# Column sums of a 256 MB array: eight running rows with one VectorE add a load and a small GpSimd add, in place of four running rows with two VectorE adds a load

## The chip, the cores and the metric

The kernel runs on one core of a Trainium2 chip. The metric is the device time in microseconds of one execution. The engines that matter here are VectorE (DVE in the profile), GpSimd (POOL), TensorE (PE) and ScalarE (ACT); SyncE (SP) computes nothing and issues the transfers from HBM to SBUF.

## The reference

```python
batch, seq, dim = 32, 1024, 2048
grad_output = np.random.randn(batch, seq, dim).astype(np.float32)

def reference(grad_output):
    return np.sum(grad_output, axis=(0, 1)).astype(np.float32)
```

The input is 32768 rows of 2048 float32 numbers, 268.4 MB. The result is one row of 2048 column sums. Every byte is read once, and there is one addition for each number read.

## The kernel before

**Tiling.** SBUF has 128 partitions. A *row group* is 128 input rows, one on each partition, 2048 columns wide (1.05 MB); the input has 256 row groups. Three ring slots (`ring`, `SLOTS`) of 128 x 16384 columns hold eight row groups each (`M`). All loads go through the one queue of SP, in the order in which the program issues them (`load`, line 57). A load into a slot waits until the instructions that use the slot's old content are done; the framework places these semaphore waits, and the order of the instructions on each engine is the order of the program (`tc.manual_schedule()`).

**The chain (lines 90 to 99).** There are 29 loads of eight row groups (8.39 MB each), into slots 0, 1, 2, 0 and so on. The running sum is four row groups wide and lives in the first half of the newest slot. For each load VectorE does two adds of 8192 columns by `plus` (line 62): the running sum of the slot before into the first half of the new slot (line 98), and the second half of the new slot into its first half (line 99). The first of the two frees the slot before, into which load i+2 then goes.

**The tail (lines 102 to 135).** After the chain 24 row groups are left: a load of eight into slot s8, one of seven into s7, two of three into parts of the slot `run`, which also holds the running sum, three of one row group without its last 256 columns (line 113, columns up to `C` = 1792), and three of those last 256 columns (line 117). VectorE folds what it has in place by halves (`fold`): the running four rows to one, s8 to one, s7 to two, and one add of two rows of `run`. TensorE then sums over the partitions: `sums` (line 79) is a *row pass*, four matmuls that multiply one row group by a column of ones and add to the PSUM tile `acc`. There are eleven such passes, in a fixed order that ends with the late row groups, and then twelve small matmuls for the last 256 columns into `accr` (line 135).

**The end.** ScalarE copies `acc` to SBUF (line 147), ScalarE and GpSimd copy a part of it each (line 150), VectorE adds `accr` (line 154), and three small transfers store the result.

Of the kernel before, what the change touches and what calls it, by code (L numbers as in the profile page):

```python
# [1 line left out]

# [4 lines left out]

P = 128
M = 8
SLOTS = 3  # L10
CHAIN = 29
B = 256
LATE = 3


@with_exitstack
def kernel(
    ctx: ExitStack,
    tc: tile.TileContext,
    grad_output: bass.AP,  # L20
    out: bass.AP,
):

    nc = tc.nc
    f32 = mybir.dt.float32
    D = out.shape[-1]
    flat = grad_output.rearrange("b s d -> (b s) d")
    Q = D // 4
    H = B // 2
    C = D - B
    add = mybir.AluOpType.add

    sb = ctx.enter_context(tc.tile_pool(name="sb", bufs=1))
    ps = ctx.enter_context(tc.tile_pool(name="ps", bufs=1, space=bass.MemoryType.PSUM))
    ring = [sb.tile([P, M * D], f32, name=f"ring{s}") for s in range(SLOTS)]
    ones = sb.tile([P, 1], f32, name="ones")
    res = sb.tile([P, Q], f32, name="res")
    joint = sb.tile([P, C - 2 * Q], f32, name="joint")
    acc = ps.tile([P, 512], f32, name="acc")
    accr = ps.tile([P, 512], f32, name="accr")
    q, v, t, a, p = nc.sync, nc.vector, nc.tensor, nc.scalar, nc.gpsimd

    row = 0

    def load(s, at, m):

        nonlocal row
        src = flat[row * P : (row + m) * P].rearrange("(p m) d -> p (m d)", p=P)
        q.dma_start(out=ring[s][:, at * D : (at + m) * D], in_=src)
        row += m

    def plus(s, to, n, s2, of):  # L60
        part = ring[s][:, to * D : (to + n) * D]
        v.tensor_tensor(out=part, in0=part, in1=ring[s2][:, of * D : (of + n) * D], op=add)  # L62

    def fold(s, m, left):
        while m > left:
            n = m // 2
            plus(s, 0, n, s, m - n)
            m -= n

    def shares(x):  # L70


        ends = x[:, 2 * Q :].rearrange("p (b g c) -> p g b c", g=2, c=H)
        return [x[:, :Q], x[:, Q : 2 * Q], ends[:, 0], ends[:, 1]]

    def sums(s, at, w=D):
        for g, x in enumerate(shares(ring[s][:, at * D : at * D + w])):
            o = acc[32 * g : 32 * g + 1, : Q if g < 2 else (w - 2 * Q) // 2]
            t.matmul(  # L79
                o if g < 2 else o.rearrange("p (b c) -> p b c", c=H),  # L80
                lhsT=ones[:],
                rhs=x,
                start=False,
                stop=False,
                tile_position=(0, 32 * g),
                skip_group_check=True,
            )

    with tc.manual_schedule():
        for i in range(CHAIN):  # L90
            s = i % SLOTS
            load(s, 0, M)
            if i == 0:
                v.memset(ones[:], 1.0)  # L94
                v.memset(acc[:], 0.0)  # L95
                v.memset(accr[:], 0.0)  # L96
            else:
                plus(s, 0, 4, (i - 1) % SLOTS, 0)
            plus(s, 0, 4, s, 4)


        run, s8, s7 = (s, *((s + k) % SLOTS for k in (1, 2)))
        load(s8, 0, 8)
        fold(run, 4, 1)
        load(s7, 0, 7)
        fold(s8, 8, 1)
        load(run, 4, 3)
        fold(s7, 7, 2)
        plus(run, 4, 1, run, 5)
        load(run, 1, 3)  # L110
        tail = flat[row * P :]
        for k in range(3):
            q.dma_start(
                out=ring[s8][:, (1 + k) * D : (1 + k) * D + C], in_=tail[k * P : (k + 1) * P, :C]
            )
        for k in range(LATE):
            q.dma_start(
                out=ring[s8][:, 4 * D + k * B : 4 * D + (k + 1) * B],
                in_=tail[k * P : (k + 1) * P, C:],
            )  # L120
        sums(run, 6)
        sums(run, 0)
        sums(s8, 0)
        sums(s7, 0)
        sums(s7, 1)
        for at in (1, 2, 3):
            sums(run, at)
        sums(s8, 1, C)
        sums(s8, 2, C)
        sums(run, 4)  # L130
        sums(s8, 3, C)
        for k in range(LATE):
            for g in (2, 3):
                x = 4 * D + k * B + (g - 2) * H
                t.matmul(  # L135
                    accr[32 * g : 32 * g + 1, :H],
                    lhsT=ones[:],
                    rhs=ring[s8][:, x : x + H],
                    start=False,
                    stop=False,  # L140
                    tile_position=(0, 32 * g),
                    skip_group_check=True,
                )

        a.copy(out=res[0:97, :], in_=acc[0:97, :])  # L147
        left = joint[64:65, :].rearrange("p (b g c) -> p g b c", g=2, c=H)
        for g, copy in enumerate((a.copy, p.tensor_copy)):
            copy(  # L150
                out=left[:, g],
                in_=res[64 + 32 * g : 65 + 32 * g, : Q - H].rearrange("p (b c) -> p b c", c=H),
            )
        v.tensor_tensor(  # L154
            out=res[64:97, Q - H :], in0=res[64:97, Q - H :], in1=accr[64:97, :H], op=add
        )
        q.dma_start(out=out[: 2 * Q].rearrange("(g c) -> g c", g=2), in_=res[0:33:32, :])
        a.dma_start(out=out[None, 2 * Q : C], in_=joint[64:65, :])
        q.dma_start(
            out=out[C:].rearrange("(g c) -> g c", g=2), in_=res[64:97:32, Q - H :]  # L160
        )
# [1 line left out]
_INS = ['grad_output']  # L163
_OUTS = [((2048,), 'float32')]


# [23 lines left out]
```

## Time and profile before

| what | value |
|---|---|
| median of 3 runs | 631.58 us (629.75 to 631.66) |
| profiled execution | 630.45 us, of which the span in the trace is 628.7 us |
| VectorE busy | 531.9 us |
| TensorE matmul busy | 13.5 us |
| GpSimd busy | 0.7 us |
| input queue (q1) | 268.44 MB, 99.0% of 16 DMA engines' span |
| VectorE, 128x8192 add | 58 times, 8.69 us each |
| GpSimd, copy of 1x384 | 0.502 us |
| granted TensorE clock | 0.999 |

The span runs from the first to the last instruction of the trace; 1.75 us of the device time lie around it. In a group's line, the numbers behind the bar are the busy time in us, the mean of one instruction in ns, and the time that the engine was idle just before these instructions, with what ended it. A line of the timeline gives the start and the length in us, the engine, the line in the kernel, the operation, and the idle time before it with its releaser. A timeline line with "x4" is several instructions in one, and its length goes from the first to the last of them.

### The profile page before, as it was taken

To read this page: it belongs to the slowest core of one execution; us is meant where nothing else is said; L and a number is where in the kernel's file an instruction comes from. 1 tells how busy PE (TensorE), PEld (TensorE's weight loads), DVE (VectorE), ACT (ScalarE), POOL (GpSimd) and SP (SyncE) were. 2 spreads that over 40 slices of the span, in tenths; PEclk is the share of its full clock that TensorE was granted. 3 is DMA by queue.
4 is the path that set the end of the run, shared out by engine and by line. 5 is a ranking of instruction groups with operands and counts; after the bars stand their busy time and mean duration, and the time that the engine had idled before them with its cause. 6 is when DMAs were issued, how large, how long until landed. Compare 5 with 4: busy or idle time off the path is not lost.

```text
span 628.7 us, 443 instructions
## 1 busy us (share of the span) xinstructions
PE 13.5 (2%) x108; PEld 3.1 (0%) x108; DVE 531.9 (85%) x69; ACT 2.4 (0%) x3; POOL 0.7 (0%) x5
## 2 busy tenths in 40 slices
PE   0000000000000000000000000000000000000026
PEld 0000000000000000000000000000000000000001
DVE  0538988889888899888898888988889988889993
ACT  0000000000000000000000000000000000000000
POOL 0000000000000000000000000000000000000000
PEclk9999999999999999999999999999999999999999
DMA  9999999999999999999999999999999999999996
GB/s 400 404 463 400 467 400 467 400 467 400 467 400 467 400 467 400 467 400 467 400 467 400 467 400 467 401 463 404 463 404 463 404 463 404 459 409 459 413 411 254
DMA packets 5629, 268.48 MB, mean 427 GB/s; under 512 B 629, under 2 KB 1015, under 8 KB 1402
## 3 DMA queue, kind: packets, MB, share of 16 engines
q1 hardware_dynamic: 5624, 268.44, 99.0%
q8 instruction: 1, 0.02, 0.0%
q14 instruction: 2, 0.02, 0.0%
q10 hardware_dynamic: 2, 0.00, 0.0%
HBM read 268.44 MB, written 0.01 MB: 427 GB/s over the span
## 4 chain that ended last, share of the span: by engine, by line
issue 99%; POOLq 0%
POOLq L185 0%; POOLq L174 0%
## 5 line engine op out<-in xcount | busy, mean ns | idle before, releaser
L62 DVE TENSOR_TENSOR ring<-ring 128x8192 f32<-128x8192 f32 (+3 forms) x37 | 287.2, 7769 | 21.8 <-DMA ring<-in_grad_output_dram 20.7
L62 DVE TENSOR_TENSOR ring<-ring,ring 128x8192 f32<-128x8192 f32 x28 | 243.4, 8693 | 64.2 <-DMA ring<-in_grad_output_dram 64.2
L79 PE MATMUL acc<-ring,ones 128*1 128x512 f32 (+1 forms) x96 | 13.1, 688 | 611.3 <-DMA ring<-in_grad_output_dram 609.5
L154 DVE TENSOR_TENSOR res<-res,accr 33x128 f32<-33x128 f32 x1 | 0.3, 293 | 6.4 <-ACT res L147 6.4
L79 PEld LDWEIGHTS acc<-ring,ones 128*1 128x1 f32 x96 | 2.6, 90 | 620.8 <-issue 615.6
L147 ACT COPY res<-acc 97x512 f32<-97x512 f32 x1 | 0.6, 587 | 621.6 <-PE acc L79 621.6
L147 ACT ACT_TABLE_LOAD x1 | 1.3, 1283 | 1.5 <-DVE acc L95 1.5
L150 POOL COPY joint<-res 1x384 f32<-1x384 f32 x1 | 0.5, 502 | 624.6 <-ACT res L147 624.6
L135 PE MATMUL accr<-ring,ones 128*1 128x128 f32 x12 | 0.8, 272 | 0.0
L94 DVE MEMSET ones<- 128x1 f32 x1 | 0.1, 59 | 0.8 <-PEq L174 0.8
L95 DVE MEMSET acc<- 128x512 f32 x1 | 0.5, 485 | 0.1
L135 PEld LDWEIGHTS accr<-ring,ones 128*1 128x1 f32 x12 | 0.5, 84 | 0.5 <-DMA ring<-in_grad_output_dram 0.2
L96 DVE MEMSET accr<- 128x512 f32 x1 | 0.5, 485 | 0.1
L150 ACT COPY joint<-res 1x384 f32<-1x384 f32 x1 | 0.5, 507 | 0.0
L174 POOL MEMSET const-bfloat16-1.0<- 128x1 bf16 x1 | 0.1, 102 | 0.0
L174 POOL MEMSET const-uint8-127<- 128x1 uint8 x1 | 0.1, 100 | 0.0
L174 POOL MEMSET const-float32-0.0<- 128x1 f32 x1 | 0.1, 99 | 0.2 <-issue 0.2
L174 POOL MEMSET const-float32-1.0<- 128x1 f32 x1 | 0.1, 99 | 0.0
## 6 DMA issues: line engine op xcount, KB each, us to landing
ring<-in_grad_output_dram SPq DMA_DIRECT2D x1, 7168.0 KB, 27.5
ring<-in_grad_output_dram SPq DMA_DIRECT2D x2, 3072.0 KB
ring<-in_grad_output_dram SPq DMA_DIRECT2D x3, 896.0 KB, 16.1
ring<-in_grad_output_dram SPq DMA_DIRECT2D x30, 29.9
ring<-in_grad_output_dram SPq DMA_DIRECT2D x3, 128.0 KB, 16.6
out_dram<-res SPq DMA_DIRECT2D x1, 4.0 KB
out_dram<-joint ACTq DMA_DIRECT2D x1, 3.0 KB
out_dram<-res SPq DMA_DIRECT2D x1, 1.0 KB
```

Source lines behind the costliest of these rows:

```text
L62: v.tensor_tensor(out=part, in0=part, in1=ring[s2][:, of * D : (of + n) * D], op=add)
L79: t.matmul(o if g < 2 else o.rearrange("p (b c) -> p b c", c=H), lhsT=ones[:], rhs=x, start=False, stop=False, tile_position=(0, 32 * g), ...
L94: v.memset(ones[:], 1.0)
L95: v.memset(acc[:], 0.0)
L96: v.memset(accr[:], 0.0)
L135: t.matmul(accr[32 * g : 32 * g + 1, :H], lhsT=ones[:], rhs=ring[s8][:, x : x + H], start=False, stop=False, tile_position=(0, 32 * g), sk ...
L147: a.copy(out=res[0:97, :], in_=acc[0:97, :])
L150: copy(out=left[:, g], in_=res[64 + 32 * g : 65 + 32 * g, : Q - H].rearrange("p (b c) -> p b c", c=H),)
L154: v.tensor_tensor(out=res[64:97, Q - H :], in0=res[64:97, Q - H :], in1=accr[64:97, :H], op=add)
L174: nc = _bacc.Bacc("TRN2", target_bir_lowering=False, num_devices=1)
```

## The change

In the chain the running sum becomes eight row groups wide, the whole slot. For loads 1 to 22 VectorE does one add of 15360 columns (7.5 row groups) from the slot before into the new slot, and GpSimd does the same for the other 1024 columns (`SHARE` = 0.5 row groups). Both have to be done before the slot before is free. Load 0 has no add. From load 22 on (`NARROW`) the running sum is narrowed by one row group a load, from eight to four at load 25, by an add within the new slot; from load 23 on GpSimd has no part.

In the tail, s8 is folded to two row groups by VectorE and to one by GpSimd; the load into `run` behind it has four row groups instead of three, and the next one two instead of three; s7 is folded to one row group instead of two; two adds instead of one join three rows of `run`. The late row groups lie one place further on in s8. There are ten row passes instead of eleven.

```diff
+SHARE = 0.5
+NARROW = 22
...
-    def plus(s, to, n, s2, of):
-        part = ring[s][:, to * D : (to + n) * D]
-        v.tensor_tensor(out=part, in0=part, in1=ring[s2][:, of * D : (of + n) * D], op=add)
+    def plus(s, to, n, s2, of, engine=nc.vector):
+        a, b, c = int(to * D), int(of * D), int(n * D)
+        part = ring[s][:, a : a + c]
+        engine.tensor_tensor(out=part, in0=part, in1=ring[s2][:, b : b + c], op=add)
...
     with tc.manual_schedule():
+        runs = M
         for i in range(CHAIN):
             s = i % SLOTS
+            before = (i - 1) % SLOTS
             load(s, 0, M)
             if i == 0:
...
+                continue
+            if runs == M:
+                plus(s, 0, M - SHARE, before, 0)
+                plus(s, M - SHARE, SHARE, before, M - SHARE, p)
             else:
-                plus(s, 0, 4, (i - 1) % SLOTS, 0)
-            plus(s, 0, 4, s, 4)
+                plus(s, 0, runs, before, 0)
+            if i >= NARROW:
+                runs = max(4, runs - 1)
+                plus(s, 0, M - runs, s, runs)
...
         fold(run, 4, 1)
         load(s7, 0, 7)
-        fold(s8, 8, 1)
-        load(run, 4, 3)
-        fold(s7, 7, 2)
+        fold(s8, 8, 2)
+        plus(s8, 0, 1, s8, 1, p)
+        load(run, 4, 4)
+        fold(s7, 7, 1)
         plus(run, 4, 1, run, 5)
-        load(run, 1, 3)
+        plus(run, 4, 1, run, 6)
+        load(run, 1, 2)
...
-        sums(run, 6)
+        sums(run, 7)
         sums(run, 0)
         sums(s8, 0)
         sums(s7, 0)
-        sums(s7, 1)
-        for at in (1, 2, 3):
-            sums(run, at)
-        sums(s8, 1, C)
+        sums(run, 1)
+        sums(run, 2)
         sums(s8, 2, C)
+        sums(s8, 3, C)
         sums(run, 4)
-        sums(s8, 3, C)
+        sums(s8, 4, C)
```

## The prediction

> **What bounds the kernel now.** I read the page's shares by engine first, then the DMA lines, then the wait lists of VectorE and of SP, and last VectorE's timeline, because the last decides what slack a load has.
>
> ```profile
> PE 13.5 (2%) x108; PEld 3.1 (0%) x108; DVE 531.9 (85%) x69; ACT 2.4 (0%) x3; POOL 0.7 (0%) x5
> ...
> q1 hardware_dynamic: 5624, 268.44, 99.0%
> ...
> HBM read 268.44 MB, written 0.01 MB: 427 GB/s over the span
> ...
> L62 DVE TENSOR_TENSOR ring<-ring 128x8192 f32<-128x8192 f32 (+3 forms) x37 | 287.2, 7769 | 21.8 <-DMA ring<-in_grad_output_dram 20.7
> L62 DVE TENSOR_TENSOR ring<-ring,ring 128x8192 f32<-128x8192 f32 x28 | 243.4, 8693 | 64.2 <-DMA ring<-in_grad_output_dram 64.2
> ```
>
> SP's queue is busy for 99.0% of the span, VectorE for 85%; VectorE's idle time is ended by transfers. The input queue is the bound. (The alternating 400 and 467 GB/s of the page's slices are a matter of counting: a slice of 15.7 us holds six or seven of a DMA engine's 64 KB packets, 400 or 467 GB/s over 16 engines.) VectorE's timeline gives the beat:
>
> ```profile
> 0.73 50.40 SPq L57 DMA_DIRECT2D ring<-in_grad_output_dram  x4
> ...
> 22.67 8.69 DVE L62 TENSOR_TENSOR ring<-ring 128x8192 f32<-128x8192 f32 x1 [20.67 <-DMA ring<-in_grad_output_dram]
> 42.09 8.69 DVE L62 TENSOR_TENSOR ring<-ring,ring 128x8192 f32<-128x8192 f32 x1 [10.72 <-DMA ring<-in_grad_output_dram]
> 50.81 8.69 DVE L62 TENSOR_TENSOR ring<-ring 128x8192 f32<-128x8192 f32 x1
> ```
>
> ```profile
> 546.49 8.69 DVE L62 TENSOR_TENSOR ring<-ring,ring 128x8192 f32<-128x8192 f32 x1 [1.94 <-DMA ring<-in_grad_output_dram]
> 555.21 35.19 SPq L57 DMA_DIRECT2D ring<-in_grad_output_dram  x4
> ...
> 565.84 8.69 DVE L62 TENSOR_TENSOR ring<-ring,ring 128x8192 f32<-128x8192 f32 x1 [1.93 <-DMA ring<-in_grad_output_dram]
> 574.57 44.00 DVE L62 TENSOR_TENSOR ring<-ring 128x8192 f32<-128x8192 f32 x9
> 605.46 1.28 SPq L113 DMA_DIRECT2D ring<-in_grad_output_dram  x3
> ```
>
> Two numbers carry everything below. The **beat**: the first add of each load starts every 19.35 us (546.49 to 565.84; nearly every interval of the timeline is 19.34 to 19.36), 8.39 MB at 433 GB/s. The **round trip on an empty queue**: the first load is issued at 0.73 and its add starts at 22.67, so 21.94 us. It is 2.59 more than a beat, hidden as long as the next load is issued early. A load is issued 0.03 us after the add that frees its slot (546.49 + 8.69 = 555.18, issue at 555.21). That add ends 8.7 us into the beat, so the queue never runs dry.
>
> **The change, part by part.**
>
> *The slot comes free later.* With T(i) as the time at which load i's add may start, load i+2 goes into the slot that the add of load i reads. Its data is ready at the later of T(i+1) + 19.35 (queue full) and T(i) + add + 0.03 + 21.94 (queue empty). Before, the add was 8.69: 30.7, against two beats of 38.70, 8 us to spare. After, it is one add of 15360 columns. The forms of line 62 give 8.69 us for 8192 columns and 4.43 for 4096, so 1.042 ns a column and 0.16 fixed: 16.16 us. Then 16.16 + 0.03 + 21.94 = 38.13, and **0.57 us** is left. For VectorE alone this costs nothing; its cover is that 0.57. Removing the old second add (8.69 a load) gains nothing: VectorE was not the bound.
>
> *GpSimd's 1024 columns.* They are added on the same load's semaphore, and SP's next load now waits for both engines. SP's queue is in order, so everything behind that load waits too. The trace has no two-input add on GpSimd, nor any GpSimd work beside a VectorE add with two SBUF operands, so two things are bounded. Its length, G: GpSimd's copy of 384 columns took 0.502 us and its memset of one column 0.10, so 1.05 ns a column; 1024 columns take 1.17 us if two operands cost what one does, 2.25 if each operand takes its own turn, 3.3 if the write does too. I take 2.25, the count of reads. What it adds after the end of VectorE's add: nothing if the two run side by side (then G could be 16 us and be hidden), all of G if they exclude each other, in whichever order. Below nothing it can't be: GpSimd takes no column from the 15360. I take all of G. The reason from the rows: VectorE's add runs at 1.042 ns a column in each form, reading two SBUF operands per column at a fixed pace, and GpSimd wants two more streams from the same partitions in the same microseconds. The one overlap on record speaks the other way: at 625.0 GpSimd's copy (0.502) ran under VectorE's add on line 154 and was as fast as ScalarE's same copy (0.507). That add had an operand in PSUM, so only one SBUF read, and so it is not the same case.
>
> The Trainium skill, "SBUF — State Buffer", section "Who interferes with whom", speaks against this change: a VectorE instruction with two SBUF inputs and a GpSimd instruction that reads SBUF share one read interface, and the second to start waits for the whole of the first. By that rule the sum is the forecast's; by the overlap at 625.0 it would be the first rival's, and the rule itself exempts that overlap, since it had one SBUF input. For G the skill's "GPSIMD Engine Reference", section "Elementwise — side-by-side cycle accounting", has 4497 ns for 2048 columns, half of which is an estimate of 2.25 us, and the sum would be the same.
>
> The price: T(i+2) = T(i) + 38.13 + 2.25 = 40.38 instead of 38.70, 1.68 per two loads, 0.84 per load. (Only half of the excess counts, because two loads are in turn: after a late load the next comes a full beat behind it.) GpSimd takes part in the adds of loads 1 to 22, so loads 3 to 24 are late: 22 x 0.84 = **18.5 us**.
>
> *Narrowing, loads 22 to 25.* VectorE does 16.16 + 2.29, 15.10 + 4.43, 12.96 + 6.55, 10.83 + 8.69, so up to 19.5 us against a beat of 19.35: a lag of some tenths, absorbed by 17.4 a load after that. Slots come free at 15.10 or sooner, 37.1 against 38.70. Cost 0, hidden by the transfers.
>
> *The tail.* Bytes are the same (256 row groups). VectorE drops the last fold of slot s8 (2.29, given to GpSimd) and takes two more single-row adds (4.58): its end moves from 618.57 to 620.86, counted at the old beat. PE has ten passes of about 0.43 us instead of eleven, off the path. The last transfers, whose arrival lets PE go on at 623.28, set the end; the row summed just before them, run row 4, needs VectorE's last add and 0.43 of PE, so 623.28 - 0.43 - 620.86 = 1.99 us are spare. GpSimd's 2048-column add becomes ready at 603.2, while VectorE has adds without pause. If they run side by side: 0. If they exclude each other, VectorE's chain is 4.4 us longer (2 x 1.05 x 2048 + 0.10), which is **2.4 us** past the spare. If GpSimd instead waits for VectorE's last add, PE's queue stands at its third pass until 625.3; eight passes (3.4) and the last twelve matmuls (0.8) follow, 629.5 instead of 624.4: 5.1. I take 2.4. The last six loads are issued at 603.2 instead of 605.5, which buys nothing, since their data is not due before about 616.
>
> Sum: 630.45 (profiled execution, its span of 628.70 and 1.75 around it) + 18.5 + 2.4 = 651.4. The median of the runs is 631.58, 1.1 higher; I put the forecast at 652.0, between the two bases.
>
> **Rivals.**
>
> 1. *Side by side, no change.* If SBUF serves both engines, the 0.57 us of slack holds and every load arrives on its beat: 630.4 to 631.6. For it: the overlap at 625.0, and VectorE with 85% on a queue that is 99% busy. Against it: two SBUF operands on each side. It decides at what GpSimd adds to the 16.16: up to 0.57 us it wins, beyond that the forecast's recurrence takes over.
> 2. *Partial clash.* GpSimd steals one VectorE cycle for each of its columns: 1024 x 1.042 = 1.07 us, (1.07 - 0.57) / 2 x 22 = 5.5; in the tail 2.13 against 1.99 spare, 0.1: 636. Full exclusion with G = 1.17 comes to the same region: 6.6 and 0.3, 637. Nothing in the rows favours it over the ends.
> 3. *Faster.* Side by side, and two irregularities of this trace do not come back: the intervals at 42 to 101 us are 0.6 us over the beat in sum, and one at 391 to 411 us is 20.04, 0.69 over. A slot freed with fewer instructions on VectorE could be why, though neither has a VectorE row to blame: 630.45 - 1.3 = 629.1, 0.4% below the median. Nothing more is to be had while the bytes and the beat stay.
>
> That the change doesn't do what it says is not a case of its own: the instruction order shows 22 adds of 15360 columns on VectorE and 22 of 1024 plus one of 2048 on GpSimd.
>
> **Chances.** A difference of 0.3% (1.9 us) is about what a measurement of this kernel can tell from none. Full exclusion, 641 to 658 by G from 1.5 to 2.75: 0.56. Partial, 634 to 641: 0.12. Side by side, 629.7 to 633.5: 0.26. Faster: 0.05. G above 2.75, up to 3.3 (30 us on the loads and 4.7 in the tail, 665): 0.01. So slower 0.69, same 0.26, faster 0.05. The range from 629.5 to 657 leaves out little more than the ends of both; the likeliest case's own range is 641 to 658.
>
> **What would show it.** Right: the starts of VectorE's long adds alternate between about 21.0 and 19.35 us apart; SP's loads (line 59 of the changed kernel) wait for POOL (or for a VectorE add that shows 18.4 instead of 16.16); GpSimd's add ends about 18.4 us after the load landed; q1's share falls to about 96%. Wrong, first rival: GpSimd's adds end within the 16.16 us, VectorE's group means 16.2, the beat stays 19.35. Wrong in its base: a round trip on an empty queue that is not 21.94 in mid-run, which would show as late loads with GpSimd long done. In the tail, VectorE or POOL as the last wait of PE ahead of the last copy means that the tail's price is real; a transfer there means that it is 0.

## The result, and the profile after

The median went from 631.46 us (629.75 to 631.66) to 652.85 us (652.5 to 653.91), a ratio of 1.0346 with a 95% interval of 1.0327 to 1.0365. The forecast was 652.0. The profiled execution took 652.76 us, span 650.5 (before: 630.45, span 628.7). Ratios here and below leave out runs more than 1.5% above the fastest of their kernel, which is one run, 662.53 us in run 7. As the runs below show, the sum came out well although one of its steps was wrong.

The page of the changed kernel, shares by engine, input queue, and the two groups of line 65 that share the loop's work:

```profile
PE 13.0 (2%) x92; PEld 2.9 (0%) x92; DVE 511.4 (79%) x48; ACT 2.4 (0%) x3; POOL 414.4 (64%) x28
...
q1 hardware_dynamic: 5624, 268.44, 96.8%
...
L65 DVE TENSOR_TENSOR ring<-ring,ring 128x15360 f32<-128x15360 f32 (+4 forms) x28 | 420.4, 15016 | 128.2 <-DMA ring<-in_grad_output_dram 127.9
L65 POOL TENSOR_TENSOR ring<-ring,ring 128x1024 f32<-128x1024 f32 x22 | 402.9, 18315 | 80.3 <-DMA ring<-in_grad_output_dram 80.3
```

VectorE does less (511.4 us instead of 531.9), the queue is idle more, and 1024 columns keep GpSimd "busy" for 18.3 us. The timeline shows what that number is:

```profile
61.42 16.16 DVE L65 TENSOR_TENSOR ring<-ring,ring 128x15360 f32<-128x15360 f32 x1 [3.18 <-DMA ring<-in_grad_output_dram]
61.46 18.31 POOL L65 TENSOR_TENSOR ring<-ring,ring 128x1024 f32<-128x1024 f32 x1 [1.02 <-DMA ring<-in_grad_output_dram]
82.28 16.16 DVE L65 TENSOR_TENSOR ring<-ring,ring 128x15360 f32<-128x15360 f32 x1 [4.70 <-DMA ring<-in_grad_output_dram]
82.32 18.31 POOL L65 TENSOR_TENSOR ring<-ring,ring 128x1024 f32<-128x1024 f32 x1 [2.54 <-DMA ring<-in_grad_output_dram]
101.61 16.16 DVE L65 TENSOR_TENSOR ring<-ring,ring 128x15360 f32<-128x15360 f32 x1 [3.17 <-DMA ring<-in_grad_output_dram]
```

Both engines start on the same load within 0.04 us; VectorE is not slowed (16.16, as reckoned), GpSimd ends 2.19 us after it. The starts are 20.86 and 19.33 us apart in turn, and from load 1 (42.09) to load 21 (445.73) two loads take 40.36 us on average. SP's wait list (us in total, times, longest) names the late release, 2.17 us behind VectorE each time:

```profile
SPq L59 <- DVE ring L65: 547.1, 30, 56.2
SPq L59 <- POOL ring L65: 47.8, 22, 2.2
```

The tail of the changed kernel:

```profile
583.66 8.69 DVE L65 TENSOR_TENSOR ring<-ring,ring 128x8192 f32<-128x8192 f32 x1 [1.92 <-DMA ring<-in_grad_output_dram]
...
592.39 50.51 DVE L65 TENSOR_TENSOR ring<-ring 128x8192 f32<-128x8192 f32 x10
620.95 1.29 SPq L126 DMA_DIRECT2D ring<-in_grad_output_dram  x3
621.00 10.76 POOL L65 TENSOR_TENSOR ring<-ring 128x2048 f32<-128x2048 f32 x1 [137.37 <-DVE ring L65]
...
638.42 7.30 PE L82 MATMUL acc<-ring,ones 128*1 128x512 f32 x54 [3.47 <-DVE ring L65]
...
640.09 0.15 PEld L82 LDWEIGHTS acc<-ring,ones 128*1 128x1 f32 x4 [0.71 <-issue]
640.94 0.15 PEld L82 LDWEIGHTS acc<-ring,ones 128*1 128x1 f32 x4 [0.71 <-issue]
...
646.23 0.59 ACT L159 COPY res<-acc 97x512 f32<-97x512 f32 x1 [643.41 <-PE accr L147]
```

GpSimd waits through VectorE's add of 6144 columns (6.55) and then works for 4.2 us, while VectorE's next add waits. TensorE, held up by VectorE until 638.42, never waits again. The pause of 3.47 us before it has a price too. Each matmul of the program shows as two instructions, so a group of four weight loads (x4) is half a row pass. The half passes behind the pause begin up to 0.86 us apart, from 641.69 on 0.43. By the table of stretches the clock granted to TensorE was 0.57 in the first 4 us behind the pause (the column after the busy times):

```profile
638.00:642.00 4.00, 3.58 (x20) 0.64 (x24) 3.96 (x3) 0.00 (x0) 0.00 (x0) 0.57 0.69 264
642.00:646.00 4.00, 4.00 (x52) 1.53 (x44) 0.90 (x1) 0.00 (x0) 0.00 (x0) 1.00 0.00 1
```

Four half passes took 3.27 us (638.42 to 641.69) instead of 1.72, so 1.55 us were lost. In the traces of the kernels here such slow half passes follow pauses of 3.4 to 4.4 us (also in runs 1, 8 and 12), and none follows the pause of 1.8 us before. TensorE's very first passes (from 609.5 before, from 629.7 here) are as slow, although the clock column reads 1.00 there. The same place before:

```profile
616.42 7.89 PE L79 MATMUL acc<-ring,ones 128*1 128x512 f32 x72 [1.78 <-DVE ring L62]
...
624.39 0.59 ACT L147 COPY res<-acc 97x512 f32<-97x512 f32 x1 [621.57 <-PE acc L79]
```

The books: load 28's add starts at 583.66 instead of 565.84, **17.8 us** for the loop. From there to the copy out of PSUM it is 62.57 us instead of 58.55, **4.0 us** for the tail. Together 21.8, the difference of the spans.

### The profile page after: what moved, and what is told of

Its sections match the earlier page's. It is cut to its first block, busy times and chain, and to the rows that moved or that the text cites. A ratio compares the mean times of both kernels' runs of the same rounds, so it can differ in the third digit from the quotient of the medians.

```text
span 650.5 us, 440 instructions
## 1 busy us (share of the span) xinstructions
PE 13.0 (2%) x92; PEld 2.9 (0%) x92; DVE 511.4 (79%) x48; ACT 2.4 (0%) x3; POOL 414.4 (64%) x28
## 4 chain that ended last, share of the span: by engine, by line
DMA 48%; POOL 31%; DVE 19%; PE 1%; issue 0%; POOLq 0%; ACT 0%; SPq 0%; DVEq 0%
DMA ring<-in_grad_output_dram 48%; POOL ring L65 31%; DVE ring L65 19%; PE acc L82 1%; ACT res L159 0%; POOLq L197 0%; PE accr L147 0%; SPq L59 0%; POOLq L65 0%; DVEq L65 0%; POOLq L162 0%
## 5 line engine op out<-in xcount | busy, mean ns | idle before, releaser
L65 DVE TENSOR_TENSOR ring<-ring,ring 128x15360 f32<-128x15360 f32 (+4 forms) x28 | 420.4, 15016 | 128.2 <-DMA ring<-in_grad_output_dram 127.9
L65 POOL TENSOR_TENSOR ring<-ring,ring 128x1024 f32<-128x1024 f32 x22 | 402.9, 18315 | 80.3 <-DMA ring<-in_grad_output_dram 80.3
L65 POOL TENSOR_TENSOR ring<-ring 128x2048 f32<-128x2048 f32 x1 | 10.8, 10756 | 137.4 <-DVE ring L65 137.4
L65 DVE TENSOR_TENSOR ring<-ring 128x2048 f32<-128x2048 f32 (+3 forms) x16 | 89.7, 5619 | 2.6 <-POOL ring L65 2.2
L82 PE MATMUL acc<-ring,ones 128*1 128x512 f32 (+1 forms) x80 | 13.0, 794 | 633.2 <-DMA ring<-in_grad_output_dram 629.7
```

What stands on the lines that cost most here:

```text
L65: engine.tensor_tensor(out=part, in0=part, in1=ring[s2][:, b : b + c], op=add)
L82: t.matmul(o if g < 2 else o.rearrange("p (b c) -> p b c", c=H), lhsT=ones[:], rhs=x, start=False, stop=False, tile_position=(0, 32 * g), ...
```

## The experiments

Theory at this point: GpSimd's add and VectorE's exclude each other, so the slot is free at 18.38 us of the beat instead of 16.19. With the round trip seen here (issue at 60.47, add at 82.28: 21.81) two loads take 40.19, not 38.70. Rivals: GpSimd's add is slow by itself; VectorE's single long add is already too late. Each run is compared with runs of the kernel before on its own chip (medians there 630.0 to 631.9), and the ratio is of these.

**1. GpSimd's columns left out; 2. all columns on VectorE.**

```diff
-                plus(s, 0, M - SHARE, before, 0)            # run 2 only
+                plus(s, 0, M, before, 0)                    # run 2 only
-                plus(s, M - SHARE, SHARE, before, M - SHARE, p)
```

> GpSimd's 1024 columns of loads 1 to 22 are left out (those columns lack the rows of the loads before); VectorE's adds of 15360 columns and the whole tail stay as in the changed kernel. Exclusion (GpSimd's add runs only after VectorE's and frees the slot 2.2 us later): the slot is free at 16.19, and 16.19 + 21.81 = 38.00 is below two beats (38.70), so the 17.8 us of the loop go and the tail's 4.0 stay: 635.0 us. Rival, VectorE's long add alone comes too late: the loss in the loop stays, about 650. Rival, GpSimd's add is slow by itself: 635 as well.

> VectorE adds all 16384 columns, GpSimd none in the loop; tail as in the changed kernel. By the recurrence of two loads: release at 17.22 + 0.03, plus the round trip of 21.81 seen in the changed kernel, is 39.06 against 38.70; 0.36 / 2 x 22 loads = 4.0 us, so 639.0 us, 14 faster than the changed kernel, with VectorE's adds alternating by less than 0.4 us. Rival, the half is wrong and each load pays the whole excess: 7.9, 643. Rival, the late release is not the cause: 635 or 650.

Measured: 650.78 us, ratio 1.0336 (1.0312 to 1.0361), and 659.11 us, 1.046 (1.0443 to 1.0476). The first rival was right, VectorE's long add alone comes too late, and the theory's slack of 38.70 - 38.00 = 0.70 us does not hold: with GpSimd out of the loop and the slot free at 16.19 us, the time hardly moved. With 17.25 us it is even longer than with 18.38, which no theory had. Run 1's timeline:

```profile
140.83 16.16 DVE L65 TENSOR_TENSOR ring<-ring,ring 128x15360 f32<-128x15360 f32 x1 [3.91 <-DMA ring<-in_grad_output_dram]
157.02 40.54 SPq L59 DMA_DIRECT2D ring<-in_grad_output_dram  x3
161.04 16.16 DVE L65 TENSOR_TENSOR ring<-ring,ring 128x15360 f32<-128x15360 f32 x1 [4.05 <-DMA ring<-in_grad_output_dram]
181.04 16.16 DVE L65 TENSOR_TENSOR ring<-ring,ring 128x15360 f32<-128x15360 f32 x1 [3.84 <-DMA ring<-in_grad_output_dram]
```

A load is issued at 157.02 and its add starts at 181.04, 24.0 us later. 16.19 + 24.0 = 40.2, the beat of 20.1 that the starts show. The 24.0 is not itself the loss, because it holds the rest of the load ahead, which was used at 161.04. A full queue would have had the new load ready at 161.04 + 19.35 = 180.39, an empty one at 140.83 + 16.19 + 21.94 = 178.96. It came 0.65 us after the later of the two; over the loop it is 0.7 us a load (15.5 over 22).

Where this goes, the input queue shows. From 60 to 460 us (packets, MB, share of the 16 engines' time), before, in the changed kernel and in run 1:

```profile
q1 hardware_dynamic: 2976, 173.02, 100.0%
```

```profile
q1 hardware_dynamic: 2863, 166.66, 98.1%
```

```profile
q1 hardware_dynamic: 2879, 167.71, 99.3%
```

That is 433, 417 and 419 GB/s. In the changed kernel about half of the missing 3.7% is engines that have no packet. In run 1 that is only 0.7 of 3.1%; the rest is packets that take longer. With each packet of run 1's trace put on the engine whose last packet had just ended, an engine stands without one for 0.19 us before a load (loads 3 to 22, on average), and its first two packets of the load take 2.78 and 2.53 us instead of 2.42: 0.66 us a load in all.

How the 16 engines stand to each other, single packets tell. One row of the DMA view for each of three kernels over the same 4 us (199 to 203), in 40 slices of 0.1 us; 655 is one 64 KB packet, counted where it starts, and each of the 16 engines starts one per 2.4 us. Before:

```profile
GB/s 3277 1311 1311 655 0 0 0 0 0 0 0 0 0 0 0 0 0 0 0 0 0 0 655 2621 3932 655 1966 655 0 0 0 0 0 0 0 0 0 0 0 0
```

The changed kernel, and run 1:

```profile
GB/s 0 0 0 0 0 0 655 655 2621 1966 2621 0 0 655 655 0 655 0 0 0 0 0 0 0 0 0 0 0 0 0 0 655 655 3277 2622 655 655 0 1311 0
```

```profile
GB/s 2622 0 0 0 655 655 0 0 1966 0 655 0 0 0 655 0 0 0 0 0 0 1311 655 655 0 1311 0 1311 655 0 655 655 0 0 0 0 1311 655 0 0
```

Before, the 16 engines move in step: their packets fall within 0.6 us. In the changed kernel, within 1.1 us. In run 1 they are spread over most of the 2.4 us of a packet. A load has landed when its slowest engine has (in run 1 the engines end the load used at 161.04 between 158.80 and 160.59), and that engine also holds up the add that frees the next slot. So a load that comes when the queue is nearly empty, but not quite, may cost more than one that comes when it is empty: the new theory, which run 12 tests in part.

**3. GpSimd alone; 4. a copy; 5. a fill.** What does the exclusion depend on?

```diff
-                plus(s, 0, M - SHARE, before, 0)                                          # run 3
-                plus(s, M - SHARE, SHARE, before, M - SHARE, p)                           # runs 4, 5
+                p.tensor_copy(out=ring[s][:, cols], in_=ring[before][:, cols])            # run 4
+                p.memset(ring[s][:, int((M - SHARE) * D) : M * D], 0.0)                   # run 5
```

> VectorE's adds of 15360 columns are left out (only GpSimd's 1024 columns are summed over loads 1 to 22); the rest stays. Exclusion: with VectorE silent GpSimd's add takes 2.2 us (18.31 less 16.16, and 1.17 to 3.3 by the bounds of the prediction), the slot is free at once, 635 us. Rival, GpSimd is slow by itself: 18.3 us an add as in the changed kernel, the release as late as there, about 653 us.

> GpSimd copies the 1024 columns from the slot before instead of adding them (those columns lose the new load's rows): one SBUF operand instead of two, waiting and waited for as in the changed kernel. Exclusion by any GpSimd read: the copy ends after VectorE's add, 16.16 + about 1.2 = 17.4; 17.4 + 21.81 = 39.2, 0.5 / 2 x 22 = 5.7 us in the loop, 640.7 us, and a span of 17.3 us for each copy. Rival, only a second GpSimd operand clashes: copies of 1.2 us that end under VectorE's add, 635.0 us.

> GpSimd fills the 1024 columns with zeros instead of adding (those columns lose the rows of loads 0 to 22): it writes SBUF and reads nothing, beside the same VectorE add; the slot before does not wait for it. What counts is its span. If the whole GpSimd instruction is kept out by VectorE's add: some 17 us. If only its reads clash: 1 to 2 us, begun and ended under VectorE's add. The time is 635.0 us in both, since no release hangs on it.

Measured: 634.15 us (1.0062, 1.0042 to 1.0082), 659.35 us (1.0471, 1.0429 to 1.0513), 652.22 us (1.0325, 1.0291 to 1.0359). The groups, in the order of the runs:

```profile
L65 POOL TENSOR_TENSOR ring<-ring,ring 128x1024 f32<-128x1024 f32 x22 | 51.4, 2338 | 399.1 <-DMA ring<-in_grad_output_dram 399.1
```

```profile
L106 POOL COPY ring<-ring 128x1024 f32<-128x1024 f32 x22 | 374.7, 17031 | 112.5 <-DMA ring<-in_grad_output_dram 112.5
```

```profile
L65 DVE TENSOR_TENSOR ring<-ring,ring 128x15360 f32<-128x15360 f32 x22 | 355.5, 16158 | 122.8 <-DMA ring<-in_grad_output_dram 122.8
...
L105 POOL MEMSET ring<- 128x1024 f32 x22 | 20.9, 951 | 443.7 <-DMA ring<-in_grad_output_dram 443.7
```

GpSimd's add takes 2.34 us by itself, so "slow by itself" is out. A copy with one SBUF operand waits for VectorE as the add does; a fill, which reads nothing, runs beside VectorE in 0.95 us. Beside this add GpSimd's reads clash, its writes do not. The Trainium skill, "SBUF — State Buffer", section "Who interferes with whom", says just this of a two-input VectorE instruction and a GpSimd instruction that reads or only writes SBUF; these runs agree. As times, runs 4 and 5 missed as runs 1 and 2 did (640.7 and 635.0 were expected): their slots are free at 17.10 and 16.19 us. Run 5 is the case of two engines that do work side by side, and it is as slow as run 1.

**6. VectorE's add in two.**

```diff
-                plus(s, 0, M - SHARE, before, 0)
+                plus(s, 0, 3.75, before, 0)
+                plus(s, 3.75, 3.75, before, 3.75)
```

> VectorE's add of 15360 columns becomes two of 7680 (8.16 us each); GpSimd's add and the tail stay. Exclusion for the length of one instruction: GpSimd gets in between the two, so its span is about 8.2 + 2.2 = 10.4 us and the second VectorE add starts or ends 2.2 us late, at 18.5; the release is as late as in the changed kernel, 652.9 + 0.2 x 22 / 2, so 653 to 656 us. Rival, GpSimd has the lower right and always waits for VectorE to pause: span 18.5, VectorE untouched, the same time. Rival, slow by itself: span 18.3, VectorE untouched.

Measured: 655.24 and 660.95 us, ratio 1.0418 (1.0357 to 1.0478). The timeline of the second:

```profile
142.53 8.16 DVE L65 TENSOR_TENSOR ring<-ring,ring 128x7680 f32<-128x7680 f32 x1 [1.16 <-DMA ring<-in_grad_output_dram]
142.57 10.31 POOL L65 TENSOR_TENSOR ring<-ring,ring 128x1024 f32<-128x1024 f32 x1 [9.21 <-DMA ring<-in_grad_output_dram]
```

GpSimd gets in behind the first half (8.16 + 2.2 = 10.3), and the second takes 10.3 instead of 8.16 (the mean over both halves is 9.22). So the exclusion lasts one instruction, and either engine can be the one that waits. The time is in the expected region in one run and above it in the other. In the profiled one (660.95) two loads take 40.4 to 40.6 us up to 304 us, as in the changed kernel; from there on, with the same release, intervals of 22.5, 22.7 and 22.1 us come in between.

**7. The changed loop with the old tail; 8. the old loop with the changed tail; 9. the same without GpSimd's row.** Runs 7 and 8 exchange the tails of the two kernels as they stand; run 9 is run 8 with

```diff
-        plus(s8, 0, 1, s8, 1, p)
```

> The changed kernel's loop with the tail of the kernel before (s8 folded by VectorE alone, twelve row passes). The loop's price of 17.8 stays, the tail's 4.0 goes: 648.8 us. Rival, the tail's price comes from the loop (VectorE's lag in the narrowing): 652.8.

> The loop of the kernel before with the tail of the changed one (GpSimd adds 2048 columns of s8, ten row passes). The tail's price alone: 631.5 + 4.0 = 635.5 us, GpSimd's add with a span of about 10.8 us, and the VectorE add behind it about 8.6 instead of 4.4. Rival, no price without the loop: 631.5.

> The loop of the kernel before, the changed tail, and GpSimd's add of one row group of s8 left out (the sum lacks that row group's 128 rows). If GpSimd's reading is the tail's whole price: 631.5 us, all VectorE adds of 4096 columns at 4.4. If VectorE's two added row adds or the new order of the passes cost something: up to 4.0 more, 635.5.

Run 7 scattered: 648.29 and 648.95 us as expected, 656.89 and 662.53 in two other runs, ratio 1.0311 (1.024 to 1.0383). By itself it does not price the tail. Its loop lost 18.3 us in the profiled run (648.95). Run 8: 634.69 us, 1.0049 (1.0032 to 1.0066), 3.1 us by the ratio and 4.3 by the profiled spans (633.0 against 628.7). Run 9: 630.32 us, 0.999 (0.9979 to 1.0). So the tail's price is real without the new loop, and all of it comes with GpSimd's add: VectorE's added row adds and the new order of the passes cost nothing. Run 8's groups show where VectorE pays: three adds of 4096 columns at a mean of 5820 ns; in run 9 the mean is 4425:

```profile
L62 DVE TENSOR_TENSOR ring<-ring 128x4096 f32<-128x4096 f32 x3 | 17.5, 5820 | 0.1
```

**10. Half loads with GpSimd; 11. half loads without.** Both have the old tail.

```diff
-            load(s, 0, M)
+            load(s, 0, 4)
+            load(s, 4, 4)
...
-                plus(s, 0, M - SHARE, before, 0)
+                plus(s, 0, 4, before, 0)
+                plus(s, 4, 4 - SHARE, before, 4)            # run 11: 4 in place of 4 - SHARE, and GpSimd's add left to VectorE
```

> The changed loop with each load of eight row groups split into two of four, VectorE's add into 8192 and 7168 columns, GpSimd's 1024 columns as before; the tail of the kernel before. The first half of the slot is free 8.7 us into the beat and the second about 9.9 us after its own data came, so the exclusion stays (GpSimd spans of about 9.8 us) but no load is late: 631.5 us, or 0.5 less if fewer pauses occur. Rival, the clash costs whatever the slack of the loads: about 648.8.

> As the run with half loads, but VectorE adds all columns (8192 and 8192) and GpSimd none. Both theories of the slot: no load is late, 631.5 us, at most some tenths under the kernel before: eight running rows by themselves are worth nothing where the queue is full. Rival, fewer VectorE instructions stop the pauses of 0.6 and 0.7 us that the kernel before shows: 630.2.

Measured: 631.98 us, 1.0016 (1.0007 to 1.0026), and 631.65 us, 1.001 (1.0001 to 1.002). Run 10's group of GpSimd:

```profile
L65 POOL TENSOR_TENSOR ring<-ring,ring 128x1024 f32<-128x1024 f32 x22 | 215.2, 9781 | 244.9 <-DMA ring<-in_grad_output_dram 244.9
```

The exclusion is still there (9.78 us for an add of 2.34), and its price is gone, because no load waits for it near the end of the one ahead. The loop's loss hangs on when the slots come free, not on the exclusion itself. Nothing is gained either: half loads beat at 9.71 to 9.72 us, 19.43 a slot against 19.35, and neither run is under the kernel before. No experiment points to a version that beats it.

**12. The slot free a microsecond sooner.**

```diff
-                plus(s, 0, M - SHARE, before, 0)
-                plus(s, M - SHARE, SHARE, before, M - SHARE, p)
+                plus(s, 0, 7, before, 0)
```

> VectorE adds 14336 columns in loads 1 to 22, the other 2048 columns are left out of the sum there, GpSimd has no part in the loop; the tail is the changed one. The slot is free at 15.12, a microsecond sooner than with 15360 columns. Theory formed after the run with 15360 columns alone: a load issued within one packet's time of the end of the one ahead finds some of the 16 DMA engines already empty, they fall out of step, and the round trip of the slowest rises from 21.8 to about 24.0; then 15.12 + 24.0 = 39.1 against 38.7, 0.2 x 22 = 4.6 us at most on 635.5 (the changed tail alone), so 635.5 to 640. Packets of the 16 engines bunched within 0.7 us mean 635.5, spread over the 2.4 us between packets mean about 640. Rival, a long VectorE add as such slows the transfers: about 650, as with 15360 columns.

Measured: 634.89 us, ratio 1.0068 (1.004 to 1.0095); six of seven runs lie between 634.16 and 635.66, one at 640.05. In the profiled one load 28's add starts at 565.89 (before: 565.84): no loss in the loop at all. From issue to add its loads take 38.70 - 15.12 = 23.6 us, nearly the 24.0 of run 1, and lose nothing: here this is just the wait behind a full queue. A long VectorE add as such is out as the cause: this one takes 15.09 us, and the changed kernel, with 16.16, keeps to the recurrence. Packets over 300 to 304 us in this run:

```profile
GB/s 0 0 0 1311 655 655 655 3277 1966 0 0 1311 0 655 0 0 0 0 0 0 0 0 0 0 0 0 0 655 655 655 655 2621 3277 0 0 1311 0 655 0 0
```

They lie within 1.1 us, with a gap behind them. So neither the spread nor the loss is here; that the one makes the other, this run does not show. That the run at 640.05 was one with the engines out of step would fit the expectation's upper end; it left no trace, so this is not shown.

The loops side by side, each from one profiled execution:

| kernel | slot free after (us) | load 28's add later than before (us) |
|---|---|---|
| run 3 | 2.4 | -1.1 |
| before | 8.72 | 0 |
| run 12 | 15.12 | 0.05 |
| run 1 | 16.19 | 15.5 |
| run 5 | 16.19 | 16.3 |
| run 4 | 17.10 | 22.0 |
| run 2 | 17.25 | 24.2 |
| changed | 18.38 | 17.8 |
| run 7 | 18.38 | 18.3 |
| run 6 | 18.4 | 26.1 |

## Why the prediction was right, and where it was wrong

*The bound and the beat.* Right. Less work on VectorE gained nothing, and rival 3's price for fewer VectorE instructions did not show in run 11.

*GpSimd's add: G = 2.25, fully exclusive.* Right on both counts: 2.34 by itself, 2.19 behind VectorE's end. The estimate of 2.25 that the prediction worked out from the "GPSIMD Engine Reference" of the Trainium skill, section "Elementwise — side-by-side cycle accounting", is near what run 3 measured.

*The recurrence, 40.38 for two loads.* Right for this kernel: 40.36 on average (40.19 in the lines shown), and 17.8 us where 18.5 were forecast.

*"For VectorE alone this costs nothing; its cover is that 0.57."* **Wrong, and this is the step that failed.** The step behind it is that a load is ready at the later of two times, a beat after the load ahead or 21.94 us after its own issue. Run 1 is exactly this case, VectorE alone with the slot free at 16.19 us. Its loads come 0.7 us later than either time, and it loses 15.5 us in the loop. So rival 1 was mispriced: had the two engines run side by side, the time would not have been 630 to 632 but near the 650.78 of run 1 and the 652.22 of run 5. The forecast took the exclusion for the point that decides between no loss and 18.5 us. It is there, but over VectorE's late release alone it adds about 2 us (652.85 against 650.78).

There is luck in the number. That the changed kernel keeps to the recurrence could not be relied on: run 6, with the same release, kept to it for half of the loop, then fell behind it and lost 26.1 us in all. The last paragraph of the prediction named the sign, late loads with GpSimd long done, but gave it no case and no chance.

*The tail, 2.4 us.* The mechanism was right, VectorE's chain 4.2 us longer for GpSimd's reading (4.4 forecast), and the price was 4.0. The spare of 1.99 was reckoned at the wrong row: it was counted at run row 4, with row passes of 0.43 us. A half pass takes 0.43, a pass 0.86. The row that decides is s7's: ready 50.6 us after load 28's add before, 54.8 now. Behind it TensorE has seven passes and the small matmuls, which take 7.8 us without a wait; before, 8.0 us lay between the same two points, so the spare was 0.2. What the prediction left out is the slow start behind the pause, 1.55 us of the 7.8. Without it the spare would have been about 1.7 and the price about 2.5 (an estimate from these rows), so the 2.4 missed by about this term.

(The kernel before has twelve passes, 96 matmul instructions at eight a pass, where the text ahead says eleven; the change takes two away. The twelve small matmuls are instructions too, two for each of six calls.)

*Narrowing.* Lag without loss, as forecast: VectorE starts 19.58 to 19.59 us apart over three loads, and waits for a transfer again from load 27 on.

## What to carry to other kernels

Where a ring of slots feeds a full transfer queue, do not spend the slack down to the round trip of one load: here a slot that came free 4.2 us before the queue's next beat (19.35 less 15.12) cost nothing, and one that came 3.2 us before it cost 15.5 us, 2.5% of the time. Release parts of a slot as they are read (run 10) before taking work off the engine that reads them. And work handed to GpSimd beside a two-input VectorE add is not beside it if it reads SBUF: time it where VectorE pauses, or it moves the end of both.

## What the runs showed of the hardware that was not expected

- The loss is not set by the release time alone: a slot free after 15.12 us lost nothing, 16.19 to 17.25 lost 15.5 to 24.2 us, and about 18.4 lost 17.8, 18.3 and 26.1. In the changed kernel's trace nearly every second load finds all 16 DMA engines without a packet, and they start again together. In run 1 it is 0 to 8 of the 16 (3 on average), and the packets stay spread. Why the spread lasts, and why the first packets of a load take longer there, the traces do not tell; that the spread is the cause of the loss is read from the packets' times, not tested by itself.
- TensorE's passes took twice as long behind pauses of 3.4 us and more, which cost the changed kernel's tail 1.55 us.
- Kernels in this region scatter from run to run (648.29 to 662.53 in run 7, 656.83 to 661.91 in run 4, 655.24 and 660.95 in run 6), where the kernel before stays within 629.7 to 633.0.
- Giving GpSimd the 1024 columns, exclusion and all, was 6 us faster in these runs than leaving them to VectorE in one add (652.85 against 659.11).
